# Seven products of halves: sums built up in PSUM, copied by ScalarE, left factors made ahead

## The chip, the core and the metric

The kernel runs on one core of a Trainium2 chip. Its time is the device time of one execution in microseconds (us); the median of three executions is 1952.87 us (1952.02 to 1954.01). The profile is of one further execution of 1951.87 us, whose span, from its first to its last recorded instruction, is 1950.0 us. Engine names are those of the profile: PE is TensorE (PEld its weight loads), DVE is VectorE, ACT is ScalarE, POOL is GpSimd, SP is the queue that issues most of the transfers.

## What is computed

The reference is a two-layer generator block over 512 latent and 256 context tokens of width 1024. Each layer has three mixing branches, an output projection, and a gated feed-forward part of width 2816. In the first layer all 768 tokens go through that last part, in the second only the 512 latent ones. The change touches only the feed-forward part of the first layer:

```python
def swiglu(h, w1, w3, w2):
    return (jax.nn.silu(h @ w1) * (h @ w3)) @ w2

x = x + gt2 * swiglu(modulate(rms_norm(x, norm2[l]), sh2, sc2), w_ff1[l], w_ff3[l], w_ff2[l])
```

## The kernel before

Activations lie transposed: features on the 128 partitions, the 768 tokens along the free axis. To keep fp32 accuracy each factor is split in a rounded part `hi` and the rest `lo` (`split`: ACT casts to fp32r, then DVE or POOL subtracts), and a product is three matmuls: hi·hi, hi·lo, lo·hi.

In the first layer's feed-forward part the 22 blocks of 128 output features are taken in pairs, and the pairs in five parts (0–4, 4–8, 8–12, 12–16, 16–22 blocks). After each part its share of the product with `w_2` is added to the residual stream (`ff2_j`, evacuated at L992). The very first pair is computed plainly (`first_pair`). Each of the ten others (`ff_pair`) needs two matrix products, one with `w_ff1` (then SiLU) and one with `w_ff3` (then multiplied in). Each is a 2-by-2 block product: two halves of output features, two halves of the 1024 inputs, and two halves of 384 tokens. It is done with seven half-size products instead of eight (Strassen's method in Winograd's form), so 20 of these block products in all. One half-size product is 12 matmuls of 128 by 128 weights on 384 columns (4 blocks of inputs, 3 matmuls each).

The right factors (halves of the activations and their sums) are made once, in `arena` tiles A and B. The left factors are made for each block product by `pair_weights`: four transfers of 256 KB into `ws` tiles, four sums (`fw`, L263, DVE), and seven splits (`wh` on ACT at L224, `wl` at L225; every seventh on POOL, the others on DVE). Their buffers are five `ws`, three `fw`, and four each of `wh` and `wl`, which all other weights of the kernel use as well.

`pair_product` issues the seven products, each into a PSUM bank of its own, from eight banks in rotation (`pD` and the halves of two `wide` tiles). The first is copied out by ACT (L325); the others are added to running sums in SBUF by DVE (L328, L334, L337 and the four handlers `ev11` to `ev21`), each reading one operand from PSUM. The handlers then apply SiLU on ACT, or multiply on POOL (L949, L954, L960, L965), and `keep_u` splits the result for `w_2`.

The order on each engine is not the order of the code: a scheduler lays the instructions out by its own simulated times, respecting buffers and dependences. Every engine then runs its list strictly in order. Between the products lie background sums on DVE (`mod_sums`, L156; tiles `wm` and `junk`) that compute the modulation vectors of later stages. They are fed by 512 KB transfers on SP, each released by a small POOL copy (L180); every `pump()` issues one transfer and one or two sums.

Of the kernel before, what the change touches and what calls it, by code (L numbers as in the profile page):

```python
# [11 lines left out]
AF = mybir.ActivationFunctionType  # L12
ALU = mybir.AluOpType
# [3 lines left out]
P = 128  # L17
# [19 lines left out]
def dit_block(ctx: ExitStack, tc: tile.TileContext, xT, conds, vecs, ident_in, rope_c, rope_s,  # L37
              w_modT, w_six, w_in, w_abc, w_o, w_13, w_2, ws_t, bs, out):
    nc = tc.nc

    const = ctx.enter_context(tc.tile_pool(name="const", bufs=1))
    big = ctx.enter_context(tc.tile_pool(name="big", bufs=1))
    PBUFS = {"D": 4, "F": 1, "O": 1, "PT": 2, "st": 1, "RB": 1, "hst": 1, "KB": 1, "VT": 1, "gst": 1,
             "gT": 2, "mix": 2}
# [32 lines left out]
    def pst(tag):  # L77
        return ps.tile([P, 512], F32, tag="p" + tag, name="p" + tag, bufs=PBUFS[tag])
# [5 lines left out]
    def banks(n, tag):  # L84

        if tag != "D":
            return [pst(tag) for _ in range(n)]
        turn[0] += 1
        if n == 2:
            i = turn[0] % 3  # L90
            return [wide[i][:, 0:512], wide[i][:, 512:1024]] if i < 2 else [pst("D"), pst("D")]
        i = turn[0] % 8
        return [pst("D")] if i % 2 else [wide[i // 4][:, i // 2 % 2 * 512:i // 2 % 2 * 512 + 512]]

    def f(t):
        return t.bitcast(F32)
# [102 lines left out]
    lo_rot = [0]  # L199
# [44 lines left out]

    def pair_weights(src):

        def load(b, k0):
            t = wtile("s")  # L250
            nc.sync.dma_start(t, src[b][:, k0:k0 + 4, :].rearrange("p k n -> p (k n)"))
            return t
        a11, a21, a22, a12 = (load(*i) for i in ((0, 0), (1, 0), (1, 4), (0, 4)))

        def parts(x):
            hi, lo = wtile("h"), wtile("l")
            lo_rot[0] += 1
            split(x, hi, lo, nc.gpsimd if lo_rot[0] % 7 == 0 else nc.vector)
            return hi, lo

        def add(x, y):
            o = slot("fw", 512)
            nc.vector.tensor_tensor(o, x, y, op=ALU.add)  # L263
            return o
        f1 = add(a21, a22)
        p1 = parts(a11)
        f2 = add(f1, a11)
        p6 = parts(f2)
        p2 = parts(a12)
        p7 = parts(add(a11, a21))  # L270
        p5 = parts(f1)
        p3 = parts(add(f2, a12))
        p4 = parts(a22)
        return p1, p6, p5, p7, p2, p3, p4
# [33 lines left out]
    def pair_product(w, tmp, ev11, ev12, ev21, ev22):  # L308

        def prod(D, ww, right):  # L310
            wh, wl = ww
            for kk in range(4):
                ah, al = right(kk)
                for i, (x, a) in enumerate(((wh, ah), (wh, al), (wl, ah))):
                    nc.tensor.matmul(D, lhsT=x[:, kk * P:(kk + 1) * P], rhs=a, start=kk == 0 and i == 0,
                                     stop=kk == 3 and i == 2)

        def bank():
            return banks(1, "D")[0][:, :HT]

        p1, p6, p5, p7, p2, p3, p4 = w
        s1, u2, u3, u5 = tmp
        D = bank()
        prod(D, p1, lambda k: half_of(k, 0))
        nc.scalar.copy(s1, D)  # L325
        D = bank()
        prod(D, p6, lambda k: sum_of(1, k))
        nc.vector.tensor_tensor(u2, s1, D, op=ALU.subtract)  # L328
        D = bank()
        prod(D, p2, lambda k: half_of(k + 4, 0))  # L330
        ev11(D, s1)
        D = bank()
        prod(D, p7, lambda k: sum_of(2, k))
        nc.vector.tensor_tensor(u3, u2, D, op=ALU.add)  # L334
        D = bank()
        prod(D, p5, lambda k: sum_of(0, k))
        nc.vector.tensor_tensor(u5, u2, D, op=ALU.add)  # L337
        ev22(D, u3)
        D = bank()
        prod(D, p3, lambda k: half_of(k + 4, 1))  # L340
        ev12(D, u5)
        D = bank()
        prod(D, p4, lambda k: sum_of(3, k))
        ev21(D, u3)


    def norm_stats(X, a, b):
# [120 lines left out]
    for l in range(2):  # L468
# [79 lines left out]
        if l == 0:  # L548
            six = [wide[0][:, 0:512], wide[0][:, 512:], wide[1][:, 0:512], wide[1][:, 512:], pst("D"), pst("D")]
            RB = norm_stats(X, *XS)  # L550
            for k in range(KD):
# [4 lines left out]
                for hb in range(2):  # L556
                    w = load_piece(w_six[k][:, hb * 384:(hb + 1) * 384])
# [367 lines left out]
                if t == i == 1:  # L925
                    keep_u(su[n], U)

        def ff_pair(m, U):
# [3 lines left out]
            def silu11(D, u):  # L932
                nc.vector.tensor_tensor(a1, u, D, op=ALU.add)
                nc.scalar.activation(a1, a1, AF.Silu)

            def silu12(D, u):
                nc.vector.tensor_tensor(a2, u, D, op=ALU.add)
                nc.scalar.activation(a2, a2, AF.Silu)

            def silu22(D, u):  # L940
                nc.vector.scalar_tensor_tensor(b2, D, -1.0, u, op0=ALU.mult, op1=ALU.subtract)

            def silu21(D, u):
                nc.vector.tensor_tensor(b1, D, u, op=ALU.subtract)
                nc.scalar.activation(sb, sb, AF.Silu)

            def mul11(D, u):
                nc.vector.tensor_tensor(u, u, D, op=ALU.add)
                nc.gpsimd.tensor_tensor(a1, a1, u, op=ALU.mult)  # L949

            def mul12(D, u):
                c_ = u
                nc.vector.tensor_tensor(c_, u, D, op=ALU.add)
                nc.gpsimd.tensor_tensor(a2, a2, c_, op=ALU.mult)  # L954
                keep_u(sa, U)

            def mul22(D, u):
                c_ = tmp3[0]
                nc.vector.scalar_tensor_tensor(c_, D, -1.0, u, op0=ALU.mult, op1=ALU.subtract)
                nc.gpsimd.tensor_tensor(b2, b2, c_, op=ALU.mult)  # L960

            def mul21(D, u):
                c_ = u
                nc.vector.tensor_tensor(c_, D, u, op=ALU.subtract)
                nc.gpsimd.tensor_tensor(b1, b1, c_, op=ALU.mult)  # L965
                keep_u(sb, U)

            pair_product(pair_weights(w_13[l, 0, 2 * m:2 * m + 2]), four("tp"), silu11, silu12, silu21, silu22)
            pump()
            tmp3 = four("tp")  # L970
            pair_product(pair_weights(w_13[l, 1, 2 * m:2 * m + 2]), tmp3, mul11, mul12, mul21, mul22)
            pump()

        parts = [(0, 8), (8, 15), (15, 22)] if last else [(0, 4), (4, 8), (8, 12), (12, 16), (16, 22)]
        for pi, (f0, f1) in enumerate(parts):
            U = []
            if last:
                plain(f0, f1, U)
            else:
                for m in range(f0 // 2, f1 // 2):  # L980
                    if m:
                        ff_pair(m, U)
                    else:
                        first_pair(U)
            if f1 == NFF and not last:
                hnext = new_h()
            def ff2_j(j, sg):
                w = load_w(w_2[l, j][:, f0:f1, :], f1 - f0)

                def ev(D, a, b):  # L990
                    c = int(a >= SEQ)
                    nc.vector.scalar_tensor_tensor(X[j][:, a:b], D, MOD[l][:, 5, j, c:c + 1],  # L992
                                                   X[j][:, a:b], op0=ALU.mult, op1=ALU.add)
                gemm(w, U, sg, ev)
                if not last and f1 < NFF:
                    gate_mods[0] = X[j][:, W - 1:W]
                    pump()
                if f1 == NFF:
                    a, b = sg[0][0], sg[-1][1]
                    if last:  # L1000
                        nc.sync.dma_start(out[j], X[j][:, :SEQ])
                    else:
                        nc.sync.dma_start(xspill[j][:, a:b], X[j][:, a:b])

            if f1 == NFF and not last:
                lagged(ff2_j, segs, halves, lambda p: norm(X, G1[1], MOD[1][:, 0], *p, hnext), KD)
            else:
                for j in range(KD):
                    ff2_j(j, segs)
# [65 lines left out]
```

## Time and profile before

| | |
|---|---|
| median of 3 executions | 1952.87 us |
| profiled execution, its span | 1951.87 us, 1950.0 us |
| PE busy / PEld busy | 1868.8 us (96%) / 1644.1 us (84%) |
| DVE / ACT / POOL busy | 1178.3 / 750.5 / 868.6 us |
| block products (L315): first and last matmul | 673 and 1117 us |

PE's busy time is drawn with a modelled end of each matmul: a matmul of 384 columns is shown as 334 ns, but in a run the next one starts about 173 ns later, so busy times of neighbours overlap. An idle gap of PE is therefore shown too short, and the waits of PEld say more about how long the engine stood still.

### The profile page before, as it was taken

The page shows a single profiled execution, that of the slowest core. Times are in us where ns is not written, and L with a number is a line of the kernel's source. Part 1 is how long each engine was busy: PE and PEld are TensorE (multiplying, and loading weights), DVE is VectorE, ACT ScalarE, POOL GpSimd, SP SyncE. Part 2 cuts the span into 40 slices and gives each one's busy share as a digit, 9 for nine tenths or more (in the row PEclk, how much of TensorE's full clock was granted, in tenths as well). Part 3 has the DMA queues.
Part 4 walks back from the last instruction along what each step waited for, and adds up shares of the span by engine and source line. Part 5 has one row for each costly group of instructions (what it writes and reads, how often), then busy time and mean ns, then how long its engine had stood idle before and what let it go on. Part 6 is the DMA issues. An engine that isn't in the chain of part 4 may idle for free. (4 is left out here: it accounts for less than half of the span.)

```text
span 1950.0 us, 27698 instructions
## 1 busy us (share of the span) xinstructions
PE 1868.8 (96%) x10150; PEld 1644.1 (84%) x10150; DVE 1178.3 (60%) x1910; ACT 750.5 (38%) x1455; POOL 868.6 (45%) x724
## 2 busy tenths in 40 slices
PE   4789999999999999999999999999999999999999
PEld 3668998888889898999999988788888888888887
DVE  7877866655546969797868767459423362222222
ACT  4346766212222632322323344458432353324131
POOL 4677744545432342524333447744332254324141
PEclk9989999999999999999999999999999999999999
DMA  8833201424345034344343254400322433332302
GB/s 279 305 106 104 75 29 39 152 92 151 109 149 186 28 103 146 109 151 141 120 165 132 71 161 140 140 28 7 108 92 98 158 108 119 98 102 86 114 23 81
DMA packets 110040, 224.52 MB, mean 115 GB/s; under 512 B 12624, under 2 KB 21584, under 8 KB 109904
## 3 DMA queue, kind: packets, MB, share of 16 engines
q1 hardware_dynamic: 107840, 219.60, 34.1%
q10 hardware_dynamic: 2064, 3.15, 0.6%
q8 instruction: 80, 1.31, 0.3%
q14 instruction: 56, 0.46, 0.1%
HBM read 214.84 MB, written 5.24 MB: 113 GB/s over the span
## 5 line engine op out<-in xcount | busy, mean ns | idle before, releaser
L225 POOL TENSOR_TENSOR wl<-ws,wh 128x512 fp32r<-128x512 f32 (+2 forms) x345 | 490.9, 1434 | 462.8 <-ACT wh L224 372.2
L234 PE MATMUL wide<-A,wh 128*128 128x512 f32 (+2 forms) x1696 | 455.6, 364 | 13.1 <-ACT A L224 3.3
L234 PEld LDWEIGHTS wide<-A,wh 128*128 128x128 f32 x1696 | 293.5, 189 | 65.7 <-ACT A L224 4.5
L224 ACT CAST wh<-ws 128x512 fp32r<-128x512 f32 (+2 forms) x546 | 306.7, 604 | 68.3 <-DMA ws<-in_w 13.2
L234 PE MATMUL wide<-A,wl 128*128 128x512 f32 (+2 forms) x848 | 281.1, 364 | 2.4 <-POOL wl L225 2.1
L225 DVE TENSOR_TENSOR wl<-ws,wh 128x512 fp32r<-128x512 f32 x201 | 173.6, 865 | 132.4 <-ACT wh L224 124.6
L234 PE MATMUL pD<-A,wh 128*128 128x512 f32 (+1 forms) x784 | 234.9, 381 | 5.9 <-ACT A L224 2.8
L156 DVE SCALAR_TENSOR_TENSOR wm<-wm,fixed 128x1024 f32<-128x1024 f32 x112 | 159.4, 1426 | 32.8 <-DMA wm<-in_w_modT 31.5
L234 PEld LDWEIGHTS pD<-A,wh 128*128 128x128 f32 x784 | 145.1, 190 | 34.5 <-ACT A L224 3.2
L234 PEld LDWEIGHTS wide<-A,wl 128*128 128x128 f32 x848 | 149.1, 190 | 28.1 <-POOL wl L225 3.6
L234 PE MATMUL wide<-u,wh 128*128 128x512 f32 (+1 forms) x592 | 148.4, 352 | 0.3 <-DVE xr L992 0.3
L234 PE MATMUL pD<-A,wl 128*128 128x512 f32 (+1 forms) x392 | 147.3, 379 | 0.4 <-POOL wl L225 0.4
L234 PE MATMUL pD<-u,wh 128*128 128x512 f32 (+1 forms) x464 | 121.0, 356 | 0.0
L225 POOL TENSOR_TENSOR u<-su,u 128x768 fp32r<-128x768 f32 (+1 forms) x44 | 74.1, 1694 | 85.2 <-ACT u L224 85.2
L234 PEld LDWEIGHTS wide<-u,wh 128*128 128x128 f32 x592 | 98.7, 188 | 15.8 <-DVE xr L992 0.6
L749 POOL TENSOR_SCALAR pp<-pp,nm 128x768 f32<-128x768 f32 (+1 forms) x80 | 66.6, 833 | 101.2 <-DVE nm L748 62.6
L156 DVE SCALAR_TENSOR_TENSOR junk<-wm,fixed 128x1024 f32<-128x1024 f32 x48 | 70.5, 1468 | 61.3 <-DMA wm<-in_w_modT 60.8
L810 ACT ACTIVATE gate<-wide 128x512 f32<-128x512 f32 (+1 forms) x56 | 26.7, 516 | 196.6 <-PE wide L234 188.3
L224 ACT CAST u<-su 128x768 fp32r<-128x768 f32 (+1 forms) x44 | 32.0, 729 | 175.1 <-DVE su L889 96.4
L234 PE MATMUL wide<-u,wl 128*128 128x512 f32 (+1 forms) x296 | 91.2, 352 | 0.9 <-DVE wl L225 0.9
L234 PEld LDWEIGHTS pD<-u,wh 128*128 128x128 f32 x464 | 79.0, 188 | 12.5
L234 PEld LDWEIGHTS pD<-A,wl 128*128 128x128 f32 x392 | 74.3, 190 | 14.6 <-POOL wl L225 0.8
(254 smaller groups left out, 3763.8 us busy)
## 6 DMA issues: line engine op xcount, KB each, us to landing
ws<-in_w SPq DMA_DIRECT2D x256, 256.0 KB, 3.0
wm<-in_w_modT SPq DMA_DIRECT2D x112, 512.0 KB, 4.3
ws<-in_w_in SPq DMA_DIRECT2D x184, 256.0 KB, 3.1
ws<-in_w_o SPq DMA_DIRECT2D x48, 256.0 KB, 5.4
ws<-in_w_abc SPq DMA_DIRECT2D x32, 256.0 KB, 2.8
ws<-in_w_six SPq DMA_DIRECT2D x16, 192.0 KB, 4.9
xr<-in_xT SPq DMA_DIRECT2D x8, 384.0 KB, 7.5
ws<-in_w SPq DMA_DIRECT2D x16, 192.0 KB, 2.5
```

What stands on the lines that cost most here:

```text
L156: nc.vector.scalar_tensor_tensor(o, t, 1.0, sbc[:, c, :], op0=ALU.mult, op1=ALU.mult, accum_out=MOD[l][:, sec, b, c:c + 1])
L224: nc.scalar.copy(hi, src)
L225: (lo_eng or nc.gpsimd).tensor_tensor(lo, src, f(hi), op=ALU.subtract)
L234: nc.tensor.matmul(d[:, :b - a], lhsT=ww, rhs=aa[:, a:b], start=kk == 0 and i == 0, stop=kk == n - 1 and i == 2)
L749: nc.gpsimd.tensor_scalar(pt[:, :nk], pt[:, :nk], nm[:, 3:4], 0.0, op0=ALU.mult, op1=ALU.add)
L810: nc.scalar.activation(g_[:, a:e], D, AF.Tanh, scale=0.5)
```

## The change

Two things are rewritten.

`pair_product` uses another form of the seven products, in which the sums are built up in PSUM. Bank A takes four of the products one after the other, and ACT copies A out after the first, second and third of them (`s1`, `u2`, `u3`); the matmuls then go on adding to the same bank. Bank B takes two products, with an ACT copy (`s5`) between them, and bank C takes one. In SBUF only three sums per block product are left for DVE (four where the second factor is multiplied in, since `mul21` now multiplies on DVE straight from PSUM, instead of a DVE subtraction and a POOL multiplication). Where a bank is used again, the next product into it waits for ACT's copy.

`pair_weights` becomes a generator, `factors`, that yields one left factor at a time over all block products of a part, in the order in which they are used. `taken` keeps three of them ahead of the product that uses one. Always the last factor of the seven (`a22`) is split on POOL. The loads of the next block product are issued inside the generator, as `ws` buffers come free.

```diff
-    def pair_weights(src):
+    def factors(srcs):
...
-        f1 = add(a21, a22)
-        p1 = parts(a11)
-        f2 = add(f1, a11)
...
+        nxt = [load(0, *i) for i in ((0, 0), (1, 0), (1, 4), (0, 4))] + [load(1, 0, 0)]
+        for n in range(len(srcs)):
+            a11, a21, a22, a12, *nxt = nxt
+            yield parts(a11)
+            s1 = total(a21, a22, ALU.add)
+            yield parts(s1)
+            s2 = total(s1, a11, ALU.subtract)
+            yield parts(s2)
+            yield parts(total(s2, a12, ALU.subtract))
+            s3 = total(a11, a21, ALU.subtract)
+            nxt += [load(n + 1, 1, 0), load(n + 1, 1, 4)]
+            yield parts(s3)
+            yield parts(a12)
+            yield parts(a22, nc.gpsimd)
+            nxt += [load(n + 1, 0, 4), load(min(n + 2, len(srcs)), 0, 0)]
+
+    def taken(gen, ahead=3):
+        got = []
+        def take():
+            while len(got) <= ahead:
+                got.append(next(gen, None))
+            return got.pop(0)
+        return take
...
-        nc.scalar.copy(s1, D)
-        D = bank()
-        prod(D, p6, lambda k: sum_of(1, k))
-        nc.vector.tensor_tensor(u2, s1, D, op=ALU.subtract)
...
+        A = bank()
+        prod(A, lambda k: half_of(k, 0))
+        nc.scalar.copy(s1, A)
+        B = bank()
+        prod(B, lambda k: sum_of(0, k))
+        nc.scalar.copy(s5, B)
+        prod(A, lambda k: sum_of(1, k), True)
+        nc.scalar.copy(u2, A)
+        prod(B, lambda k: half_of(k + 4, 1), True)
+        ev12(u2, B)
+        prod(A, lambda k: sum_of(2, k), True)
+        nc.scalar.copy(u3, A)
+        ev22(u3, s5)
+        C = bank()
+        prod(C, lambda k: half_of(k + 4, 0))
+        ev11(s1, C)
+        prod(A, lambda k: sum_of(3, k), True)
+        ev21(A)
...
+            def mul22(x, y):
+                nc.vector.tensor_tensor(x, x, y, op=ALU.subtract)
+                nc.gpsimd.tensor_tensor(b2, b2, x, op=ALU.mult)
...
+            def mul21(D):
+                nc.vector.tensor_tensor(b1, b1, D, op=ALU.mult)
                 keep_u(sb, U)
```

What stands on DVE before, around the first block product of the second pair of the third part (blocks 10 and 11; `wl` are splits, `fw` sums of left factors, `tp` and `su` running sums read from the banks `pD` and `wide`, `wm` a background sum):

```order
L328 TENSOR_TENSOR tp<-tp,pD 128x384
L263 TENSOR_TENSOR fw<-ws 128x512
L933 TENSOR_TENSOR su<-tp,wide_72 128x384
L225 TENSOR_TENSOR wl<-ws,wh 128x512
L334 TENSOR_TENSOR tp<-tp,pD 128x384
L156 SCALAR_TENSOR_TENSOR wm,fixed<-wm,fixed 128x1024
L225 TENSOR_TENSOR wl<-ws,wh 128x512
L156 SCALAR_TENSOR_TENSOR wm,fixed<-wm,fixed 128x1024
L165 TENSOR_TENSOR fixed<-fixed 128x8
L170 TENSOR_SCALAR fixed<-fixed 128x8
L337 TENSOR_TENSOR tp<-tp,wide_72 128x384
L941 SCALAR_TENSOR_TENSOR su<-wide_72,tp 128x384
```

The same place in the changed kernel (L944, L951 and L947 are the handlers `silu12`, `silu11` and `silu22`, L264 the sums of left factors):

```order
L944 TENSOR_TENSOR su<-tp,pD 128x384
L225 TENSOR_TENSOR wl<-ws,wh 128x512
L951 TENSOR_TENSOR su<-tp,wide_72 128x384
L156 SCALAR_TENSOR_TENSOR wm,fixed<-wm,fixed 128x1024
L225 TENSOR_TENSOR wl<-fw,wh 128x512
L156 SCALAR_TENSOR_TENSOR wm,fixed<-wm,fixed 128x1024
L165 TENSOR_TENSOR fixed<-fixed 128x8
L264 TENSOR_TENSOR fw<-ws 128x512
L225 TENSOR_TENSOR wl<-fw,wh 128x512
L947 TENSOR_TENSOR su<-tp 128x384
L170 TENSOR_SCALAR fixed<-fixed 128x8
L225 TENSOR_TENSOR wl<-fw,wh 128x512 x2
```

Five reads of a bank in twelve rows have become two, and a third row (L947) reads two tiles of SBUF.

ACT's list at the same block product before (L325 is the copy of the first product, L934 to L945 are SiLU):

```order
L325 COPY tp<-wide_73 128x384
L224 CAST wh<-ws 128x512
L934 ACTIVATE su<-su 128x384
L224 CAST wh<-ws 128x512
L224 CAST wh<-fw 128x512
L224 CAST wh<-ws 128x512
L224 CAST wh<-fw 128x512
L938 ACTIVATE su<-su 128x384
L945 ACTIVATE su<-su 128x768
L224 CAST wh<-fw 128x512
```

And in the changed kernel (L340, L343, L345 and L349 are the copies of `s1`, `s5`, `u2` and `u3`):

```order
L340 COPY tp<-wide_73 128x384
L224 CAST wh<-fw 128x512
L343 COPY tp<-pD 128x384
L224 CAST wh<-ws 128x512
L224 CAST u<-su 128x768
L224 CAST wh<-ws 128x512
L345 COPY tp<-wide_73 128x384
L224 CAST wh<-ws 128x512
L224 CAST wh<-fw 128x512
L952 ACTIVATE su<-su 128x768
L224 CAST wh<-fw 128x512
L349 COPY tp<-wide_73 128x384
```

One copy has become four, each with one to three casts of later left factors ahead of it; the first, third and fourth of them read bank A, in `wide_73`, and PE's next product into that bank stands behind the copy.

## Rows read from the trace of the kernel before

**Rows 1.** The page: span, and busy time of each engine.

```profile
span 1950.0 us, 27698 instructions
PE 1868.8 (96%) x10150; PEld 1644.1 (84%) x10150; DVE 1178.3 (60%) x1910; ACT 750.5 (38%) x1455; POOL 868.6 (45%) x724
```

**Rows 2.** One line, L315: duration min/median/max in ns, first and last start.

```profile
L315 PE MATMUL pD<-B,wh x320: 334/334/443, 673.3 to 1116.9; 128*128 128x384 f32 x160
...
L315 PE MATMUL pD<-A,wl x120: 334/334/446, 691.0 to 1108.8; 128*128 128x384 f32 x120
```

**Rows 3.** Busy time by stretch of the stage; the column names stand in the first line.

```profile
core 0: us, PE busy (x) PEld busy (x) DVE busy (x) ACT busy (x) POOL busy (x), PEclk, DMA share, GB/s
673.00:740.00 67.00, 66.82 (x381) 62.34 (x381) 51.77 (x78) 21.54 (x37) 28.82 (x22) 1.00 0.36 115
740.00:800.00 60.00, 55.34 (x313) 53.04 (x312) 60.00 (x96) 18.33 (x32) 19.71 (x15) 1.00 0.37 123
800.00:1117.00 317.00, 315.31 (x1808) 300.85 (x1807) 250.07 (x395) 99.19 (x180) 124.50 (x107) 1.00 0.39 129
```

**Rows 4.** Waits of PEld, 673 to 1117 us: total us, times, longest us.

```profile
PEld pD L315 <- DVE wl L225: 7.5, 9, 1.8
PEld wide L315 <- DVE wl L225: 1.2, 1, 1.2
PEld wide L315 <- ACT wh L224: 0.8, 2, 0.4
PEld wide L315 <- DVE su L933: 0.6, 1, 0.6
PEld wide L315 <- DVE tp L328: 0.4, 1, 0.4
```

**Rows 5.** PE in order of time at one stall: start us, length us, what.

```profile
755.66 0.86 PE L315 MATMUL pD<-A,wh 128*128 128x384 f32 x4
758.03 0.45 PE L315 MATMUL pD<-A,wl 128*128 128x384 f32 x1 [1.51 <-DVE wl L225]
758.31 0.51 PE L315 MATMUL pD<-A,wh 128*128 128x384 f32 x2
```

**Rows 6.** DVE in order of time around the same stall.

```profile
754.07 1.21 DVE L156 SCALAR_TENSOR_TENSOR wm<-wm,fixed 128x1024 f32<-128x1024 f32 x1
755.22 1.21 DVE L156 SCALAR_TENSOR_TENSOR junk<-wm,fixed 128x1024 f32<-128x1024 f32 x1
756.83 0.54 DVE L334 TENSOR_TENSOR tp<-tp,pD 128x384 f32<-128x384 f32 x1
757.29 0.68 DVE L225 TENSOR_TENSOR wl<-fw,wh 128x512 fp32r<-128x512 f32 x1
```

**Rows 7.** DVE's groups, 740 to 800 us: count, busy us, mean ns, idle before.

```profile
L225 DVE TENSOR_TENSOR wl<-fw,wh 128x512 fp32r<-128x512 f32 x14 | 12.2, 881 | 0.0
L156 DVE SCALAR_TENSOR_TENSOR junk<-wm,fixed 128x1024 f32<-128x1024 f32 x9 | 12.0, 1335 | 0.0
L156 DVE SCALAR_TENSOR_TENSOR wm<-wm,fixed 128x1024 f32<-128x1024 f32 x9 | 10.9, 1210 | 0.0
```

**Rows 8.** DVE's groups, 673 to 1117 us.

```profile
L263 DVE TENSOR_TENSOR fw<-fw,ws 128x512 f32<-128x512 f32 x39 | 37.4, 960 | 0.0
L328 DVE TENSOR_TENSOR tp<-tp,wide 128x384 f32<-128x384 f32 x10 | 5.5, 551 | 4.2 <-PE wide L315 4.2
```

**Rows 9.** ACT's groups, 673 to 1117 us.

```profile
L224 ACT CAST wh<-fw 128x512 fp32r<-128x512 f32 x79 | 47.9, 617 | 90.7 <-DVE fw L263 87.6 <-DVE wm L156 1.6 <-DVE junk L156 1.6
L325 ACT COPY tp<-wide 128x384 f32<-128x384 f32 x10 | 4.8, 478 | 39.2 <-PE wide L315 39.1
```

**Rows 10.** ACT's longest waits, 673 to 1117 us.

```profile
ACT wh L224 <- DVE fw L263: 87.6, 20, 16.5
```

**Rows 11.** POOL's groups, 673 to 1117 us.

```profile
L225 POOL TENSOR_TENSOR wl<-ws,wh 128x512 fp32r<-128x512 f32 x30 | 49.0, 1634 | 52.5 <-ACT wh L224 52.5
L225 POOL TENSOR_TENSOR u<-su,u 128x768 fp32r<-128x768 f32 x20 | 41.6, 2098 | 3.7 <-ACT u L224 3.7
L965 POOL TENSOR_TENSOR su<-su,tp 128x384 f32<-128x384 f32 x9 | 11.6, 1294 | 1.6 <-DVE tp L964 1.6
```

**Rows 12.** PE's longest wait after the stage, 1117 to 1330 us.

```profile
PE phst L447 <- ACT hsq L443: 1.9, 1, 1.9
```

More of the change, by code (lines that the diff above doesn't have):

```diff
@@ L306, in four, with pair_product, prod @@
         return [t[:, i * HT:(i + 1) * HT] for i in range(4)]
-    def pair_product(w, tmp, ev11, ev12, ev21, ev22):
-        def prod(D, ww, right):
-            wh, wl = ww
+    def pair_product(take, tmp, ev11, ev12, ev21, ev22):
+        def prod(D, right, more=False):
+            wh, wl = take()
             for kk in range(4):
@@ L314, in prod @@
                 for i, (x, a) in enumerate(((wh, ah), (wh, al), (wl, ah))):
-                    nc.tensor.matmul(D, lhsT=x[:, kk * P:(kk + 1) * P], rhs=a, start=kk == 0 and i == 0,
-                                     stop=kk == 3 and i == 2)
+                    nc.tensor.matmul(D, lhsT=x[:, kk * P:(kk + 1) * P], rhs=a, start=not more and kk == 0 and i == 0,
+                                     stop=kk == 3 and i == 2, skip_group_check=more)
         def bank():
             return banks(1, "D")[0][:, :HT]
-        p1, p6, p5, p7, p2, p3, p4 = w
-        s1, u2, u3, u5 = tmp
-        D = bank()
-        prod(D, p1, lambda k: half_of(k, 0))
-        nc.scalar.copy(s1, D)
-        D = bank()
-        prod(D, p6, lambda k: sum_of(1, k))
-        nc.vector.tensor_tensor(u2, s1, D, op=ALU.subtract)
[L329 to L344, printed above, removed]
+        s1, s5, u2, u3 = tmp
+        A = bank()
[16 more added lines that the diff above has]
+        ev21(A)
     def norm_stats(X, a, b):
@@ L926, in first_pair, with ff_pair @@
                     keep_u(su[n], U)
-        def ff_pair(m, U):
+        def ff_pair(m, U, take):
             sa, sb = slot("su", NT), slot("su", NT)
             a1, a2, b1, b2 = sa[:, :HT], sa[:, HT:], sb[:, :HT], sb[:, HT:]
[L932 to L954, printed above, removed]
-                keep_u(sa, U)
[L957 to L965, printed above, removed]
@@ new lines, in silu12, with silu22, silu11, silu21 @@
+            def silu12(x, D):
+                nc.vector.tensor_tensor(a2, x, D, op=ALU.subtract)
+            def silu22(x, y):
+                nc.vector.tensor_tensor(b2, x, y, op=ALU.subtract)
+                nc.scalar.activation(b2, b2, AF.Silu)
+            def silu11(x, D):
+                nc.vector.tensor_tensor(a1, x, D, op=ALU.add)
+                nc.scalar.activation(sa, sa, AF.Silu)
+            def silu21(D):
+                nc.scalar.activation(b1, D, AF.Silu)
+            def mul12(x, D):
+                nc.vector.tensor_tensor(x, x, D, op=ALU.subtract)
+                nc.gpsimd.tensor_tensor(a2, a2, x, op=ALU.mult)
@@ L966, in mul21, with mul11 @@
+            def mul22(x, y):
+                nc.vector.tensor_tensor(x, x, y, op=ALU.subtract)
+                nc.gpsimd.tensor_tensor(b2, b2, x, op=ALU.mult)
+            def mul11(x, D):
+                nc.vector.tensor_tensor(x, x, D, op=ALU.add)
+                nc.gpsimd.tensor_tensor(a1, a1, x, op=ALU.mult)
+                keep_u(sa, U)
+            def mul21(D):
+                nc.vector.tensor_tensor(b1, b1, D, op=ALU.mult)
                 keep_u(sb, U)
-            pair_product(pair_weights(w_13[l, 0, 2 * m:2 * m + 2]), four("tp"), silu11, silu12, silu21, silu22)
+            pair_product(take, four("tp"), silu11, silu12, silu21, silu22)
@@ L969, in ff_pair @@
             pump()
-            tmp3 = four("tp")
-            pair_product(pair_weights(w_13[l, 1, 2 * m:2 * m + 2]), tmp3, mul11, mul12, mul21, mul22)
+            pair_product(take, four("tp"), mul11, mul12, mul21, mul22)
             pump()
@@ L979, in dit_block @@
             else:
-                for m in range(f0 // 2, f1 // 2):
+                ms = range(f0 // 2, f1 // 2)
+                take = taken(factors([w_13[l, i, 2 * m:2 * m + 2] for m in ms if m for i in range(2)]))
+                for m in ms:
                     if m:
-                        ff_pair(m, U)
+                        ff_pair(m, U, take)
                     else:
```

23 lines of the change are left out of this document (8 added, 15 removed).

## Prediction

> **What bounds the kernel now.** I read the page first: PE is busy 96% of the span, and no other engine over 60% [rows 1]. So only what makes PE work less, or stand still less, can be gained. The change leaves the matmuls as they are: 1680 of 384 columns before (the forms of L315 add up to that; the first and the last are shown [rows 2]), and 20 block products of seven products of 12 after. In a run they follow each other at about 173 ns (four of them are shown as 0.86 us: 0.334 for the last and three steps of 0.175 [rows 5]), so one product takes PE 12 x 0.173 = 2.08 us and a block product 14.5 us.
>
> So the second view is busy time by stretch [rows 3]. From 673 to 1117 us PE shows 67 - 66.82 + 60 - 55.34 + 317 - 315.31 = 6.5 us of idle time, 4.7 of it between 740 and 800, where DVE is busy 60.00 of 60.00 us. That stretch is the second of the five parts, four block products, in which the last background sums for both conditions (`wm` and `junk`) lie as well. The clock is 1.00 throughout.
>
> The third view is who waited for whom. An idle gap of PE is drawn too short, because the matmul before it is drawn past its turn. At the largest stall PE is shown idle 1.51 us, but starts run from 756.18 (755.66 and three steps) to 758.03, 1.85 us instead of 0.173, and the first step after it is 0.28 instead of 0.173 [rows 5]: 1.79 us lost. PEld's waits say that better: the five largest are 10.5 us, of which 8.7 for a `wl` from DVE, 1.0 for running sums from DVE and 0.8 for ACT [rows 4]. I take 11 us as all that the stage loses, and so as the most that can be won there.
>
> What DVE does before that stall is seen in order of time: two background sums of 1.21 us each, two reads of banks (0.54 each), and only then the `wl` [rows 6]. DVE is simply full there, and PE's next left factor is the work that comes late.
>
> **The change part by part.** *Fewer sums on DVE.* Before, each block product has seven sums that read a bank, 0.55 us each [rows 8]; a pair has 14. After it is three in the SiLU product and four in the other, of which one each reads two SBUF tiles. Five times 0.55 plus twice the SBUF form. That form at 384 columns is not in the trace; 512 columns with two SBUF inputs took 0.96 us on the mean [rows 8], or 0.68 us where it ran undisturbed [rows 6], and 384/512 of these are 0.72 and 0.51 us. I take 0.65. So DVE has 14 x 0.55 = 7.7 us per pair before and 2.75 + 1.3 = 4.05 after: 3.6 us less per pair, 36 us over the ten pairs. Beside PE's work this is worth nothing by itself; it counts only where DVE is full. In the second part there are two pairs: 7.3 us less, against 4.7 us of idle PE, about 5.7 us with what the drawing hides (some four stalls, 0.27 each). The background sums stay: 18 of them, 22.9 us, and 12.2 us of splits of sums [rows 7]. The demand there falls from 60 us to about 53 in a stretch that PE alone needs some 54 for. So DVE is no longer the bound, but it is near it, and since its list is in order, an ill-placed pair of background sums (2.4 us) can still make one factor late. I let it give back 4 of the 5.7 us.
>
> *Left factors three ahead.* The buffers remain four of `wh` and four of `wl`, so a factor can be written only when the one four products earlier has been used: before as after, three products or 6.2 us of lead at most. What changes is that the scheduler now meets them in the order of use. In the other stretches, 673 to 740 and 800 to 1117, PEld's and PE's waits leave about 5 us (11 - 5.7), much of it at the start of a part. With 3.6 us less of DVE per pair I expect half of it, 2.5 us, to go. If nothing goes the sum loses these 2.5 us; if all goes it gains as much again.
>
> *Three more ACT copies per block product.* 60 x 0.478 us = 29 us more [rows 9] on an engine that is busy 139 of 444 us in the stage [rows 3]. By itself free. But the copy is now on PE's path: a product into bank A or B that was copied must wait for the copy. Between the two lies one product in another bank, 2.08 us; the copy takes 0.48, so 1.6 us are left for what is ahead of it in ACT's list. One cast of a left factor (0.617 us [rows 9]) fits, even two do. What does not fit is a cast that itself waits for a late sum of DVE: ACT stood 87.6 us in 20 waits for `fw`, 4.4 us each [rows 10]. In the old order these had no one behind them in a hurry. Mostly the cast ahead is of a factor that PE needs later than the copy, so a late sum would now hold PE at the copy, before the factor itself is due. The old trace has no such wait: its bounds are 0 and 4.4 - 1.6 = 2.8 us in each of 20 block products, 56 us. The nearer row is the one of DVE's load: with DVE relieved the sums come earlier, so I take 1 us in all and keep the rest for a rival.
>
> *POOL.* One multiplication less per pair (10 x 1.29 us), splits as before, about one in seven at 1.63 us [rows 11]. POOL waits more than it works there; nothing.
>
> *Loads.* Still four transfers of 256 KB per block product through five `ws` buffers, the next ones behind the third sum. DMA engines are 36 to 39% busy [rows 3]: nothing, unless SP's list is held by a background transfer that waits for POOL, which it was before as well.
>
> *After the stage* the order of the second layer's start shifts a little. PE's longest wait there is 1.9 us [rows 12]; it may go or double. I take nothing and keep 2 us either way.
>
> The sum: 4 + 2.5 - 1 = 5.5 us less than the profiled execution's 1951.87 us, about 1946.4. That execution is 1.0 us under the median of 1952.87, so the median should be about 1947.4; I say 1947.
>
> **A rule against the change.** Sums and splits with two SBUF inputs took 0.68 us undisturbed and 0.88 to 0.96 on the mean, while sums with one input in PSUM stay at 0.54 to 0.55 [rows 6 to 8]. The Trainium skill (SBUF — State Buffer, Who interferes with whom) says: "A DVE instruction with two SBUF inputs contends with a GpSimd instruction that reads SBUF". The trace agrees in direction. By that rule the edit that makes `silu22` and `mul22` sums of two SBUF tiles gives part of the gain back; how much it could be at most is the third rival below.
>
> **The rivals.**
>
> *All of it goes* (0.12). DVE falls under PE's pace everywhere and ACT is never late: 11 us, 1942. For it: three products of lead, and 7.3 us against 5.7. Against: the start of each part, where four factors must be made at once.
>
> *DVE stays the bound of the second part* (0.22). The 22.9 us of background sums are bunched there, and waits only change their names: 2 us won, 1951. For it: 60.00 of 60.00 busy, with lists that wait for each other. Against: the 7.3 us.
>
> *POOL's reads block the new SBUF sums* (0.05). Each of the 20 new sums may be held for a POOL instruction of up to 2.1 us [rows 11]; the four of the second part then cost DVE up to 8.4 us, against 7.3 relieved: nothing is won, 1952 to 1953. For it: two SBUF inputs vary with what lies beside them [rows 6 to 8]. Against: POOL is busy only 20 of the 60 us there [rows 3].
>
> *ACT's copies become PE's wait* (0.13). Place: PE's second product into bank A, ACT's list ahead of L340, L345 and L349. Decided where a cast waits for DVE longer than 1.6 us past the end of the product. At one such wait of 2.8 us in six of the 20 block products it costs 17 us, less the 5.5 won: 1964, slower than before.
>
> **How the numbers follow.** A measurement of this kernel can tell about 0.2%, 3.9 us, from no change: under 1949.0 is faster, over 1956.8 slower. My forecast has 0.48, with its own range of 1944 to 1950, of which 0.06 lies within 0.2%. Faster: 0.42 + 0.12 and 0.04 of the second rival, 0.58. Same: 0.06 + 0.18 + 0.05, 0.29. Slower 0.13. The range from 1941 to 1954 takes in the first three rivals and leaves out the fourth.
>
> **What would show it.** Right: between 740 and 800 us DVE is no longer busy all the time and PE's idle time falls under 2 us; L315's waits for `wl` fall from 8.7 to 3 us or less; DVE's busy time is some 36 us less and ACT's 29 us more; waits of PE for the copies stay at about 1 us. Wrong: if PE's new matmul line waits for ACT's copies for more than 5 us, or if DVE's waits remain at over 7 us.

## The result, and the profile after

The changed kernel takes 1958.97 us (median, 1955.37 to 1961.89), the kernel before, beside it, 1954.32 us (1951.54 to 1955.89): a ratio of 1.0026 [1.0015, 1.0037]. It is slower by about 5 us where 5.5 us less was forecast, and it lies outside the forecast's range. Three single executions further down (one each of `e_turn`, `e_turn_u_dve` and `e_turn_late`) took 2322 to 4599 us; the ratios leave them out, the medians count them.

The page of the changed kernel, span and busy times [rows 1 of before]:

```profile
span 1953.6 us, 27621 instructions
PE 1868.9 (96%) x10150; PEld 1644.3 (84%) x10150; DVE 1134.3 (58%) x1840; ACT 777.8 (40%) x1515; POOL 849.8 (44%) x714
```

The engines do roughly what was counted: DVE 44 us less (36 forecast), ACT 27 us more (29), POOL 19 us less (13), PE the same. Busy time by stretch, columns as in [rows 3] (the last matmul of the block products starts at 1121.7 us here, 1117.1 before):

```profile
673.00:740.00 67.00, 65.67 (x376) 61.43 (x375) 46.11 (x69) 23.82 (x43) 22.91 (x19) 1.00 0.34 106
740.00:800.00 60.00, 56.18 (x319) 53.84 (x318) 59.97 (x93) 24.21 (x45) 19.31 (x15) 1.00 0.42 136
800.00:1131.00 331.00, 328.27 (x1866) 311.47 (x1865) 215.62 (x343) 121.30 (x228) 119.44 (x106) 1.00 0.37 123
```

DVE is still busy for 59.97 of 60 us between 740 and 800, although each pair has four or five sums fewer. PEld's waits in the stage, total, times and longest [rows 4]:

```profile
PEld wide L331 <- DVE wl L225: 3.6, 3, 2.4
PEld pD L331 <- DVE wl L225: 3.2, 4, 1.4
PEld wide L331 <- DVE xr L999: 2.1, 1, 2.1
PEld wide L331 <- ACT tp L345: 1.1, 2, 0.5
PEld wide L234 <- DVE xr L999: 0.6, 1, 0.6
PEld pD L331 <- ACT tp L343: 0.6, 1, 0.6
PEld wide L331 <- ACT tp L340: 0.5, 1, 0.5
PEld wide L331 <- ACT tp L349: 0.4, 2, 0.2
```

The waits for `wl` fell only from 8.7 to 6.8 us. New are 2.6 us for ACT's four copies; those for `xr`, which is DVE's reading of a share of `w_2`, rose from 0.6 to 2.7 us. After the stage, up to 1250 us, PE's longest waits are other ones [rows 12]:

```profile
PE wide L234 <- ACT qa L537: 2.5, 1, 2.5
PE pD L234 <- DVE acv L628: 1.5, 1, 1.5
```

From the first matmul of the block products to the last share of `w_2` (the stage's length) the trace has 499.7 us before and 501.0 after, from there to the second layer's first share 509.0 and 510.7, and the stage starts 0.6 us later: 3.5 us between the two profiled executions. That of after, 1955.37 us, is the shortest of its eight, so it shows less than the usual loss. The stage's length is what I compare below, since the time ahead of it, where nothing was changed, varied by up to 4 us.

**The largest stall** of the stage, PE in order of time:

```profile
787.26 0.34 PE L331 MATMUL pD<-A,wl 128*128 128x384 f32 x1
789.71 0.44 PE L331 MATMUL wide<-A,wl 128*128 128x384 f32 x1 [2.11 <-DVE wl L225]
```

DVE and POOL at that place:

```profile
782.05 0.54 DVE L971 TENSOR_TENSOR su<-su,pD 128x384 f32<-128x384 f32 x1
782.51 4.12 DVE L225 TENSOR_TENSOR wl<-fw,wh 128x512 fp32r<-128x512 f32 x2
...
788.98 0.68 DVE L225 TENSOR_TENSOR wl<-ws,wh 128x512 fp32r<-128x512 f32 x1
```

```profile
781.92 4.16 POOL L225 TENSOR_TENSOR u<-su,u 128x768 fp32r<-128x768 f32 x2 [0.95 <-ACT u L224]
```

The `wl` that PE waits for is made at 788.98 in 0.68 us. Ahead of it DVE spent 4.12 us on two splits of that same shape, which ended as POOL's two did, at 786.1 to 786.6 us: each engine read two SBUF tiles. The Trainium skill (SBUF — State Buffer, Who interferes with whom) says that such a DVE instruction contends with a GpSimd one that reads SBUF; the trace agrees, with 4.12 us against 2 x 0.68. At this one place 2.8 us more of DVE's time went into two splits than they take alone; that this is what the removal of sums had given is not shown.

**The wait for `xr`**, DVE in order of time ahead of the fourth part (PE's matmul into `wide` stood still until 940.3):

```profile
930.47 1.23 DVE L156 SCALAR_TENSOR_TENSOR wm<-wm,fixed 128x1024 f32<-128x1024 f32 x1 [1.29 <-DMA wm<-in_w_modT]
...
937.10 1.23 DVE L156 SCALAR_TENSOR_TENSOR wm<-wm,fixed 128x1024 f32<-128x1024 f32 x1 [0.34 <-DMA wm<-in_w_modT]
...
939.12 1.14 DVE L999 SCALAR_TENSOR_TENSOR xr<-wide,fixed,xr 128x512 f32<-128x512 f32 x2
```

```profile
940.31 0.62 PE L331 MATMUL wide<-A,wh 128*128 128x384 f32 x2 [1.80 <-DVE xr L999]
```

The bank that the new part's product gets is the one that the last product with `w_2` still occupies. DVE could have emptied it at 937 us, but a background sum that waited for its own transfer, and a sum of a left factor (0.69 us), stand ahead in its list. Before, seven banks were taken per block product; now it is three, so the rotation stands elsewhere whenever other products begin.

### The profile page after: what moved, and what is told of

The parts are those of the page before. It is cut to its first block, busy times and chain, and to the rows that moved or that the text cites. A ratio compares the mean times of both kernels' runs of the same rounds, so it can differ in the third digit from the quotient of the medians.

```text
span 1953.6 us, 27621 instructions
## 1 busy us (share of the span) xinstructions
PE 1868.9 (96%) x10150; PEld 1644.3 (84%) x10150; DVE 1134.3 (58%) x1840; ACT 777.8 (40%) x1515; POOL 849.8 (44%) x714
## 5 line engine op out<-in xcount | busy, mean ns | idle before, releaser
L225 DVE TENSOR_TENSOR wl<-ws,wh 128x512 fp32r<-128x512 f32 x195 | 168.1, 862 | 135.9 <-ACT wh L224 127.8
```

## The experiments

My theory after the result: (a) it is not DVE's load that makes a left factor late but what stands ahead of it in DVE's list, background sums above all; (b) the shifted rotation of banks costs the rest. The rivals: ACT's copies, or making factors ahead, cost it. Ratios are to the kernel before, run beside.

**Which half of the change.** `e_psum_only`: the new sums in PSUM, the left factors made as before, per block product.

```diff
-            pair_product(take, four("tp"), silu11, silu12, silu21, silu22)
+            pair_product(pair_weights(w_13[l, 0, 2 * m:2 * m + 2]), four("tp"), silu11, silu12, silu21, silu22)
```

> The new sums in PSUM, but each block product's seven left factors made at its own start, as before the change. The scheduler's lists of PE, DVE, ACT, POOL and SP come out the same, row by row, as those of the full change. Theory (the change is only the PSUM half): the time of the full change, 0.1 to 0.4% slower than the kernel before. Rival (making factors three ahead is worth something by itself): it differs from the full change by more than 2 us.

1958.74 us, 1.0020 [1.0010, 1.0031]. The lists of all five engines are, row by row, those of the full change: on top of the new sums, "three ahead" moves nothing. I take it that the four buffers of `wh` and `wl` and the scheduler had led to that order already; no run shows the reason. Its profile is a second one of the same program, with a stage of 504.2 us instead of 501.0. The stall for `xr` is larger in it:

```profile
941.46 0.79 PE L315 MATMUL wide<-A,wh 128*128 128x384 f32 x2 [3.44 <-DVE xr L982]
```

Two background sums ahead of the reading had waited longer for their transfers, 2.72 and 0.61 us instead of 1.29 and 0.34 (DVE in order of time), and behind the stall the granted clock (third column from the end) falls:

```profile
931.40 1.23 DVE L156 SCALAR_TENSOR_TENSOR wm<-wm,fixed 128x1024 f32<-128x1024 f32 x1 [2.72 <-DMA wm<-in_w_modT]
...
938.30 1.23 DVE L156 SCALAR_TENSOR_TENSOR wm<-wm,fixed 128x1024 f32<-128x1024 f32 x1 [0.61 <-DMA wm<-in_w_modT]
...
940.27 1.14 DVE L982 SCALAR_TENSOR_TENSOR xr<-wide,fixed,xr 128x512 f32<-128x512 f32 x2
```

```profile
941.00:945.00 4.00, 3.54 (x12) 3.54 (x13) 3.43 (x8) 0.00 (x0) 1.73 (x2) 0.59 0.45 128
```

In the changed kernel's own profile it is 1.00 there. The 3.44 - 1.80 = 1.6 us of longer stall and about 4 x 0.41 = 1.6 us of slower clock are the 3.2 us between the two stages: how late two transfers land makes this difference between two executions of one program.

`e_ahead_only`: the old form of the seven products, with the generator that makes its factors three ahead (`pair_product` calls `take()` for each).

```diff
-        prod(D, p1, lambda k: half_of(k, 0))
+        prod(D, lambda k: half_of(k, 0))
```

> The old products, each in a bank of its own, with left factors from the generator, three ahead, the last of seven always on POOL. Theory: the buffers limited the lead before as well, so within 0.15% of the kernel before (under 3 us either way), with waits for DVE's splits of 7 to 10 us. Rival (the lead is what relieves): those waits under 4 us and 4 us or more won.

1956.28 us, 1.0012 [1.0003, 1.0021]. With the old products the generator does move DVE's list, and the waits for `wl` are 6.7 us, as in the full change but without any of its relief of DVE; a gain did not come. In its profile the stage is 499.1 us long, 0.6 less than before: one stall of 2.05 us is followed by a granted clock of 0.58 over 4 us, which costs 1.7 us. Behind the stage it loses 1.9 us (510.9 instead of 509.0).

**The rotation of banks.** `e_turn`: four added to the counter after each block product, so that it stands where it did.

```diff
         ev21(A)
+        turn[0] += 4
```

> The change, with the counter that hands out banks moved on by four more after each block product, so that the products with w_2 and the second layer's start get their banks in the old rotation. Theory (the bank rotation is what costs): the 2.1 us wait of a block product for an evacuation of the residual stream goes, the second layer's start has no 2.5 us wait for ACT's cast of q, and the kernel is 3 to 5 us faster than the change, about the time of before. Rival (waits of the stage only change names with any new order): within 2 us of the change, other waits of the same total of 10 to 13 us.

1955.36 us, 1.0007 [0.9998, 1.0016], against 1958.74 us of `e_psum_only` on the same chip: 3.4 us back. The wait for `xr` is gone from PEld's list and the 2.5 us for `qa` from PE's, but `wl` stays:

```profile
PEld pD L331 <- DVE wl L225: 7.0, 8, 1.6
```

So (b) accounts for most of the loss. What is left, 0.0007, can't be told from no change. (In this profile the stage is 500.2 us long. From there to the second layer's first share it takes 510.6 us, as in the changed kernel, but with the clock at 0.98 between 1500 and 1600 us instead of 1.00.)

**ACT's copies.** `e_copy_dve`: the four copies on DVE (one of four edits shown).

```diff
-        nc.scalar.copy(s1, A)
+        nc.vector.tensor_copy(s1, A)
```

> The change with the four copies of running sums done by DVE instead of ACT. If ACT's copies are what takes back the gain, their waits (3.5 us of weight loads) go and it is 2 us or more faster than the change. If DVE is what is late, 80 more reads of a bank at about 0.5 us (40 us) bring DVE's load back to the old level: waits for DVE's splits rise from 7 to 9 us or more and it is 1 to 5 us slower than the change.

1967.67 us, 1.0071 [1.0058, 1.0083], the stage 515.7 us. The copies now stand in the fuller list:

```profile
PEld wide L331 <- DVE tp L349: 5.3, 4, 2.0
...
PEld wide L331 <- DVE tp L345: 2.2, 3, 1.1
```

The waits for the copies are 8.3 us in all here, and 2.6 on ACT: ACT is the better place for them. The waits for `wl` did not rise, as expected, but fell to 2.2 us, and 8.7 us slower than the change is more than the 5 expected. ACT's copies alone are not what takes back the gain, since the loss goes with the rotation; but their 2.6 us (2.3 in `e_turn`) are more than the 1.9 us that the change wins on `wl`, so they stay a part of the account.

**The background sums.** `b_narrow` and `a_narrow`: before and after, with the background sums of the first layer's feed-forward part taken over 256 of the 1024 columns. The modulation vectors of later stages are then not the reference's.

```diff
-            nc.vector.scalar_tensor_tensor(o, t, 1.0, sbc[:, c, :], op0=ALU.mult, op1=ALU.mult,
+            nn = 256 if in_ff[0] else 1024
+            nc.vector.scalar_tensor_tensor(o[:, :nn], t[:, :nn], 1.0, sbc[:, c, :nn], op0=ALU.mult, op1=ALU.mult,
```

> The kernel before, its background sums in the first layer's feed-forward part over 256 of 1024 columns only (so the later modulation vectors are not the reference's); transfers and order rules as before. Theory (DVE's background sums in front of the splits are what makes left factors late): the waits for DVE's splits in the stage fall from 8.7 us to 3 or less, 5 to 8 us faster than before. Rival (the splits are late because of what POOL, ACT or the buffers do): at least 6 of the 8.7 us stay.

> The change, with the same background sums over 256 of 1024 columns. Theory: the waits for DVE's splits fall from 6.8 us to 3 or less as well, 4 to 7 us faster than the change; so both forms stand nearly level without the background sums (within 4 us), and the seven sums that the change takes from DVE are worth little. Rival (the relief of DVE is worth the 5.5 us forecast once something else is out of its way): 4 us or more faster than the old form with the same narrow sums.

1946.17 us, 0.9955 [0.9943, 0.9966], and 1946.88 us, 0.9966 [0.9954, 0.9978]. PEld's waits for `wl`, in `b_narrow`:

```profile
PEld pD L317 <- DVE wl L227: 0.5, 2, 0.3
```

and in `a_narrow`, with those for two copies:

```profile
PEld pD L333 <- DVE wl L227: 1.4, 1, 1.4
PEld wide L333 <- ACT tp L347: 1.1, 2, 0.5
PEld pD L333 <- ACT tp L345: 0.6, 1, 0.6
```

The stage is 490.2 and 492.4 us long. With short background sums both forms lose little (PEld's waits are 1.8 and 4.9 us in all) and are level, though DVE is busy for 323.4 us in `b_narrow` and 278.1 in `a_narrow` (673 to 1131 us): 45 us less on DVE win nothing there. It is the background sums that make PE wait. Whether by their load or by their place these two runs don't tell, since they also take 45 us from DVE.

`a_narrow` is some 12 us faster than the change, where 4 to 7 were expected. Its waits for `xr` are 0.4 us instead of 2.7, although its banks rotate as in the change. That fits a rotation that costs where a long background sum stands ahead of the reading; no run separates it further.

**Their place.** `e_turn_spread`: `e_turn`, with two background sums or pairs after each block product, and fewer in the shares of `w_2`.

```diff
-            pump()
+            pump(2)
...
-                    pump()
+                    if j % 4 == 0:
+                        pump()
```

> The change with the old bank rotation (four added to the bank counter), and with the background sums spread: two pumps after each block product, and in the products with w_2 only two per part instead of eight. Same sums in all. Theory (bunched background sums hold the splits): no stretch of the stage with DVE full, waits for DVE's splits 7 us to 3 us or less, 3 to 6 us faster than the same without spreading, and so about 2 to 4 us faster than the kernel before. Rival (any order has its own 7 us of waits): within 2 us of the one without spreading.

1964.16 us, 1.0050 [1.0036, 1.0063]: the expectation failed, and so did its rival. The waits for `wl` doubled to 14.3 us, with DVE busy for 324.1 us from 673 to 1131 us and 328.8 in `e_turn`. The load is the same, so the place decides; the sums stand between the splits in more parts now.

`b_late` and `e_turn_late`: none after the shares of `w_2`, one after each block product, and the remaining 28 sums beside the second layer's gates.

```diff
-            if not last:
-                gate_mods[0] = f(hi[:, W - 1:W])
-                pump(4)
+            gate_mods[0] = f(hi[:, W - 1:W])
+            pump(4)
...
                     gate_mods[0] = X[j][:, W - 1:W]
-                    pump()
```

> The kernel before, with the background sums placed elsewhere: none is issued any more after the shares of the product with w_2 (32 places), only after each block product (20 places), and the rest, 28 sums for one condition, beside the gates of the second layer (four after each of its merged blocks). No work is left out. Theory (the stage loses time where background sums stand in front of a split): the first layer's part carries 36 sums (16 pairs and 4 single ones) instead of 64, none of them in the stretches where a new part's factors are made, so the waits for wl fall from 8.7 us to 2 to 5 us; the second layer's gates have room (DVE 33 to 49 per cent busy), so at most 1 us is lost there: 1948 to 1951 us, 0.997 to 0.999 of before. Rival (the sums cost the same wherever they stand): the waits for wl fall as much, but as much is lost in the second layer, 1953 to 1957 us.

> The changed kernel with the old bank rotation, and the background sums placed as in the other kernel of this pair: 20 places after the block products, the rest beside the second layer's gates. No work is left out. Theory (once the sums are out of the way the two forms of block products are level): 1948 to 1951 us, within 0.1 per cent of the other kernel. Rival (lower DVE load decides): this one is faster than the other by 3 us or more, since it has 36 us less on DVE in the same stage.

1951.89 us, 0.9990 [0.9982, 0.9999], and 1958.56 us, 1.0025 [1.0016, 1.0035]. `b_late` is the only version with all the work that beats both, and by little (1948 to 1951 us were expected). The second half of the expectation failed: the two are not level, and the one with less work on DVE is the slower. One place explains much of that. DVE in `e_turn_late`, at the first new factors of a block product:

```profile
1097.49 1.23 DVE L156 SCALAR_TENSOR_TENSOR wm<-wm,fixed 128x1024 f32<-128x1024 f32 x1 [2.43 <-DMA wm<-in_w_modT]
...
1098.76 1.23 DVE L156 SCALAR_TENSOR_TENSOR wm<-wm,fixed 128x1024 f32<-128x1024 f32 x1
...
1100.98 0.68 DVE L225 TENSOR_TENSOR wl<-ws,wh 128x512 fp32r<-128x512 f32 x1
```

PE there, and the granted clock (the column behind POOL's) by stretch:

```profile
1101.72 0.45 PE L331 MATMUL pD<-A,wl 128*128 128x384 f32 x1 [2.41 <-DVE wl L225]
```

```profile
1102.00:1106.00 4.00, 4.00 (x15) 4.00 (x15) 2.03 (x4) 2.03 (x4) 0.00 (x0) 0.57 0.07 18
1106.00:1110.00 4.00, 4.00 (x25) 4.00 (x25) 1.77 (x3) 1.86 (x4) 0.00 (x0) 1.00 0.14 29
```

DVE had nothing to do for 2.43 us, with the split that PE needs four instructions further down its list, because a sum ahead of it waited for its transfer. PE stood still for 2.41 us, and then ran at 0.57 of its clock on the mean of 4 us (15 records of matmuls instead of 25): another 4 x 0.43 = 1.7 us, an estimate. In `b_late` the same sums stand behind the splits:

```profile
1098.50 0.68 DVE L225 TENSOR_TENSOR wl<-ws,wh 128x512 fp32r<-128x512 f32 x1
1099.10 1.21 DVE L156 SCALAR_TENSOR_TENSOR wm<-wm,fixed 128x1024 f32<-128x1024 f32 x1
```

Their transfer had landed at 1098.24 us, by then, and PE waited only 0.2 us there. `e_turn_spread` has the stall of `e_turn_late` as well (a sum's wait of 2.57 us, PE idle 2.52, the clock then 0.72 over 4 us).

`b_late_free` and `e_turn_late_free`: the same, with an edit that was to let transfers go as a buffer comes free, without POOL's copy.

```diff
+        gate_mods[0] = None
         for pi, (f0, f1) in enumerate(parts):
...
-                    gate_mods[0] = X[j][:, W - 1:W]
```

> The kernel before with the background sums placed late (as in the run b_late), and their transfers no longer released by a small POOL copy in the first layer's feed-forward part: a transfer goes as soon as one of the three wm buffers is free. No work is left out. Theory (a sum that stands in DVE's list ahead of a split and waits for its own transfer is what makes the split late; the transfer waited for POOL's copy): DVE's waits for wm and junk from DMA fall from 29 us in 7 to under 10, PEld's waits for wl from 3.4 us to under 2: 1949 to 1951 us. Rival (the weights' transfers are now held up by the earlier background transfers on SP, or nothing changes since the sums themselves fill the time): 1952 to 1956 us, with waits for DMA on the weights' casts.

> The changed kernel with the old bank rotation, late background sums (as in the run e_turn_late), and their transfers not released by POOL. There one stall of 2.57 us at 1099 us stood behind two sums that had waited 2.43 us for their transfer, which POOL had released late. Theory: that stall and the half clock behind it go, DVE's waits for background transfers fall from 46 us in 13 to under 15, PEld's waits for wl from 10.0 us to 4 to 6: 1950 to 1953 us. Rival (where the sums stand decides, not when their data comes): waits for wl stay at 8 us or more, 1956 to 1959 us.

1953.97 us, 1.0007 [0.9998, 1.0016], and 1957.48 us, 1.0017 [1.0009, 1.0026]. The edit does not do what both expectations suppose. It clears the gate once, ahead of the five parts, and `keep_u` sets it again each time it splits a result for `w_2` (`gate_mods[0] = f(hi[:, W - 1:W])`). POOL's copies in `e_turn_late`, and below them in `e_turn_late_free`, from 673 to 1131 us:

```profile
L180 POOL COPY wm<-u 128x1 f32<-128x1 f32 x16 | 7.8, 506 | 0.0
L180 POOL COPY wm<-xr 128x1 f32<-128x1 f32 x4 | 2.0, 510 | 108.9 <-DVE xr L999 108.9
```

```profile
L180 POOL COPY wm<-u 128x1 f32<-128x1 f32 x20 | 8.3, 443 | 0.0
```

All 20 are still there; only the four that waited for a share of `w_2` (`xr`) wait for such a split (`u`) instead. So neither theory nor rival is tested by these two runs. DVE's longer waits for background transfers are still 27.7 and 37.2 us (29.0 and 46.4 in `b_late` and `e_turn_late`), and the stall is where it was (3.07 us of PE in the second). Its trace tells who is late there, POOL, SP's queue and DVE in order of time:

```profile
1093.46 1.26 POOL L180 COPY wm<-u 128x1 f32<-128x1 f32 x2
```

```profile
1094.14 1.06 SPq L153 DMA_DIRECT2D wm<-in_w_modT  x2
```

```profile
1097.99 1.23 DVE L156 SCALAR_TENSOR_TENSOR wm<-wm,fixed 128x1024 f32<-128x1024 f32 x1 [2.71 <-DMA wm<-in_w_modT]
```

SP waited 9.0 us for the copy, which stood behind POOL's two splits of `u` (4.09 us from 1089.43). The transfer went 0.03 us after the first copy ended, and took 3.75 us to land; in `e_turn_late` the one at the same place took 3.47, and the median of the kernel before is 3.6. So the transfer is not slow at this place: it is released late, and by POOL. What a kernel without these copies would take, no run shows.

**Sharing with POOL.** `e_turn_u_dve`: in `e_turn`, the split of the products for `w_2` on DVE instead of POOL.

```diff
-            split(su, hi, lo)
+            split(su, hi, lo, None if last else nc.vector)
```

> The change with the old bank rotation, and the splits of the SwiGLU results (768 columns, POOL 2.1 us each) on DVE instead of POOL, 22 of them at about 0.95 us. If POOL's long reads are what holds DVE's splits, two such splits in a row no longer take 4.1 us of DVE, the waits for splits fall to 4 us or less, and it is 1 to 4 us faster than without. If DVE's load decides, 21 us more on DVE make it 1 to 5 us slower.

1963.75 us, 1.0049 [1.0035, 1.0063]. The waits for `wl` stay at 7.0 us. DVE's 80 `wl` made from sums, first in `e_turn`, then here:

```profile
L225 DVE TENSOR_TENSOR wl<-fw,wh 128x512 fp32r<-128x512 f32 x80 | 68.7, 862 | 5.9 <-ACT wh L224 5.8
```

```profile
L225 DVE TENSOR_TENSOR wl<-fw,wh 128x512 fp32r<-128x512 f32 x80 | 58.9, 742 | 6.2 <-ACT wh L224 5.0 <-issue 1.2
L225 DVE TENSOR_TENSOR u<-su,u 128x768 fp32r<-128x768 f32 x22 | 21.0, 974 | 3.7 <-ACT u L224 3.6
```

Without these reads of POOL beside them the splits are shorter by 0.12 us each, but 22 splits of 0.97 us now stand in DVE's list. DVE's busy time in the stage is the same (328.8 and 327.8 us), and PE waits more (`su` 2.1, L349 2.0, L340 2.4 us). Here, moving work into the list that PE waits on costs more than leaving it on POOL beside DVE's splits.

## Why the prediction was wrong

**The step that failed** is "fewer sums on DVE": I let it give back 4 of the 5.7 us in the second part. The waits for `wl` fell by 1.9 us in all, and in `e_turn`, with the same relief, by 1.7; in `e_ahead_only`, without it, they fell by 2.0. So no run shows the relief to be worth anything. I read "60.00 of 60.00 busy" as a full engine. It was a window cut around the fullest part of the list. In the 22 us behind it, to the end of that part, DVE was busy only 10.3 us before and 4.9 after:

```profile
740.00:822.00 82.00, 70.28 (x111) 1.00 0.34 112
```

```profile
740.00:822.00 82.00, 64.91 (x100) 1.00 0.38 122
```

Before, 10.5 us of that stretch are one wait of a background sum for its transfer. So DVE was not full. It runs its list as early as it can: the time that was relieved went into what came next (23 splits of factors instead of 20 within the 60 us, 19 background sums instead of 18), and the idle time behind it grew. What stands ahead of a late factor stayed. Across the runs DVE's load (busy from 673 to 1131 us) does not order PEld's waits for `wl`:

| run | DVE busy, us | waits for `wl`, us |
|---|---|---|
| before | 368.4 | 8.7 |
| `b_late` | 333.6 | 3.4 |
| `e_turn` | 328.8 | 7.0 |
| `e_turn_spread` | 324.1 | 14.3 |
| `b_narrow` | 323.4 | 0.5 |
| `e_turn_late` | 293.5 | 10.0 |

The least load of these has more waits than the greatest, and three runs within 6 us of load have 0.5, 7.0 and 14.3 us of waits.

**Left factors three ahead** were priced at 2.5 us. On the new sums the edit does nothing: identical lists. On the old ones it moves DVE's list, and nothing is won (`e_ahead_only`). I had written that the buffers limit the lead "before as after", and should have compared the order of the half alone before I gave it a price.

**ACT's copies** were priced at 1 us; it is 2.6, in six waits of at most 0.6. The mechanism and the order of size were right; the rival of 17 us stayed away.

**Banks** were not in the sum at all. That a counter is turned three times instead of seven times per block product can be read in the code; it cost 3.4 us by `e_turn`. "After the stage" I had kept 2 us either way: PE's waits to 1250 us went from 1.9 + 0.5 to 2.5 + 1.5, and came back to 1.1 + 0.5 with the old rotation.

**POOL's reads against the new SBUF sums** (the rule against the change and the third rival): the new sums of two SBUF tiles were not held. Their means are 0.55 us, like the sums that read a bank, and less than the 0.65 I took:

```profile
L962 DVE TENSOR_TENSOR tp<-tp 128x384 f32<-128x384 f32 x10 | 5.5, 555 | 4.8 <-ACT tp L349 4.6
L947 DVE TENSOR_TENSOR su<-tp 128x384 f32<-128x384 f32 x10 | 5.5, 551 | 0.2
```

What varied were the splits, from 0.68 to 2.33 us in the stage. (The 2.1 us that I gave as POOL's longest is a mean [rows 11].)

**Right** were the matmuls (nothing changed), DVE's and ACT's busy times roughly, and the loads at nothing. Of the signs that I named, DVE's waits over 7 us came true: 6.8 for `wl` and 2.7 for `xr`. Of the rivals, "DVE stays the bound of the second part", whose waits only change their names, came nearest; I gave it 0.22 and 2 us won. The sum as measured, in the profile of after: 1.9 us won on `wl` and 2.1 on other waits of PEld that are gone or smaller (those of [rows 4] below the first two, and smaller ones), 2.6 lost on copies and 2.1 more on `xr` (0.6 of its 2.7 was there before): 0.7 lost by the waits. The stage is 1.3 us longer, 1.7 are lost behind it, and 0.6 ahead of it, where nothing was changed. The usual execution loses more at `xr`: in the second profile (`e_psum_only`) the stage is 4.5 us longer than before and 0.6 us are lost behind it.

`e_turn_late` trails `b_late` by 6.7 us. Its stage is 5.9 us longer (502.4 and 496.5): PEld's waits in it are 11.6 against 8.0 us, and the half clock behind the one stall costs 1.7, together 5.3 us more. Open is what stands ahead of its other nine waits for `wl` (7.3 of its 10.0 us), and what POOL's release of the transfers costs in all.

## What to carry to other kernels

Where PE sets the pace, lowering another engine's load is worth only what it takes out from in front of the instructions that PE waits for: read that engine's list just ahead of each stall, not its busy share in a window that you cut. A rewrite that takes fewer buffers or banks from a rotation moves every later use; compare which bank stands where at the seams. When an edit is meant to change the order, see whether the lists change at all before pricing it; when it is meant to take instructions out, count them in the trace before you read the time.

## What I had not expected of the hardware

- In the changed kernel two DVE splits of 128x512 took 4.12 us beside two POOL splits of 128x768, and 0.68 us each alone; DVE's longest in the stage is 2.33 us.
- The length of a stall did not tell whether the granted clock falls behind it. In the 4 us from the stall's end it was 0.50 to 0.69 on the mean, so for much of it at 1.2 GHz, after stalls of PE of 3.44 (`e_psum_only`), 3.29, 2.53 and 2.30 (`e_turn_spread`), 2.49 (`e_copy_dve`), 2.43 and 1.81 (`e_turn_u_dve`), 2.41 (`e_turn_late`), 2.05 (`e_ahead_only`) and 1.95 us (`e_turn_late_free`). It stayed at 1.00 (2.4 GHz) after 3.07 (`e_turn_late_free`), 2.11 and 1.80 (the change) and 2.10 us (`e_psum_only`). Where it fell, 12 to 16 records of matmuls stand in those 4 us instead of 23: at 0.173 us each, 1.2 to 1.9 us on top of what the waits show (an estimate).
- Matmuls that add to a bank after ACT has copied it out of the middle of an accumulation follow at the usual 173 ns; the copy itself took 0.48 us for 128x384.
